# Completing the chunk inverses two heads at a time, with a stationary operand of 128 by 128

## The chip, the cores and the metric

The kernel runs on one core of one Trainium2 chip. The metric is the device time of one execution in microseconds (us), of which the median of several runs is given.

## The reference

The reference is a two-layer backbone over 2048 latent tokens and 256 context tokens with 1024 channels. The first layer projects the tokens and runs two groups of heads side by side: a bidirectional gated delta rule (four heads of 128) and grouped-query attention (four heads of 128, two key and value heads), then an output projection. The second layer is a convolution module. What the change touches is the triangular solve of the gated delta rule, which the reference writes for each chunk and head as

```python
lower = jnp.where(strict, jnp.einsum('bhnid,bhnjd->bhnij', kb, k) * decay, 0.0)
tmat = jnp.eye(GDN_CHUNK, dtype=q.dtype) + lower
u = lax.linalg.triangular_solve(tmat, v * beta[..., None], left_side=True, lower=True)
w = lax.linalg.triangular_solve(tmat, kb * jnp.exp(g)[..., None], left_side=True, lower=True)
```

followed by a scan over the chunks that carries a 128 by 128 state per head, once forward and once backward.

## The kernel before

The kernel works in stages. Projections come first. Then `gdn_products` makes the decayed products of all 18 chunks of 128 tokens and stores them in DRAM, and `gdn_subst` inverts their diagonal blocks of 32 by substitution on VectorE and GpSimd (tiles `sbC` and `sbT`); its last passes run into the next stage. That next stage, `layer0_mix`, runs attention and the delta rule side by side. The output projection and the second layer follow.

In `layer0_mix`, `merge` takes steps of two generators in turn: `attention`, and `gdn_all`, which itself alternates between the two directions d = 0 and 1. Each direction goes through the 18 chunks in its order. While `gdn_chain` does the chain of one chunk (matmuls into `pk`, `py`, `pq`, `pn`, `pa`), `gdn_inverse` completes the inverse of the next one, so there are 36 inverses in all, and `gdn_final` finishes the output of the last. The build then orders the instructions of each engine by a simulated timeline, starting from the order in which the generators emitted them; on the chip each engine works through its list in that order, and so groups of one operation can be broken up by work of another.

`gdn_inverse` holds a chunk's four heads in tiles with 128 partitions. It starts with the inverses of the diagonal blocks of 32 in `W` and doubles the block size twice (levels s = 32 and 64). At each level it forms, head by head, a product of an off-diagonal block `nt` (at level 32 a copy of its columns, `ntc`) with `X`, the transposed inverse, into PSUM tile `psq`; copies the wanted blocks out to `q = self.qz[d, s]`, whose other blocks were zeroed once in `zero_q`; multiplies by the diagonal blocks of `W` into `psw`; and writes the negated blocks back into `W`. Between the levels it transposes the 64 by 64 blocks of `W` into `pst` and copies them into a new `X`. The copies out of `psq` run on VectorE, those out of `psw` and `pst` on ScalarE. All matmuls here are fp32; each leaves two records in the trace, a transpose leaves one. Attention's matmuls use fp32 split into two F32R parts, with one record each.

All PSUM tiles of the delta rule come from the pool `ps_g` with three buffers. Attention has `ps_s` (scores, two buffers, evicted into `S` by VectorE) and `ps_t` (transposed probabilities `pt`, two buffers, read by ScalarE into `phi` and by VectorE into `plo`), and one buffer for the product `po`.

Of the kernel before, what the change touches and what calls it, by code (L numbers as in the profile page):

```python
# [8 lines left out]
F32 = mybir.dt.float32  # L9
# [5 lines left out]
PSUM = bass.MemoryType.PSUM  # L15
DRAM = bass.MemoryType.DRAM

P = 128
# [7 lines left out]
H = 4  # L26
# [80 lines left out]
class Build:  # L107
# [13 lines left out]
                return  # L121
            self.layer0_out_layer1()

# [1 line left out]
    def col(self, name, j=0, n=None):  # L125
        o, w = COLS[name]
        n = 1 if n is None else n
# [20 lines left out]
    def rsqrt(self, out, src, n):  # L148
        self.nc.gpsimd.tensor_tensor(out=out, in0=src, in1=self.mhalf[:, 0:1].to_broadcast([P, n]), op=ALU.pow)  # L149

# [1 line left out]
    def setup(self, es):  # L152
        tc, nc = self.tc, self.nc
        self.kp = kp = es.enter_context(tc.tile_pool(name="keep", bufs=1))
# [33 lines left out]
        self.d_sz = d("d_sz", [8, P, T])  # L188

    def ada_start(self, layer, conds, half, raws, pspool, ap, st):  # L190
        """Scale and shift columns {cond: (A[128,4], B[128,4])} of four channel tiles."""
        nc = self.nc
        nc_ = len(conds)
        rows = []
# [38 lines left out]
        return r  # L233

    def make_hT(self, xs, A, B, hi, lo, st, tp, cts=range(KT), bufs=3):
        """xs: token tiles [128,1024] scaled by rstd; writes hi/lo [128 ch, 8, n*128]."""
        nc = self.nc
        n = len(xs)
        for ct in cts:
            ps = tp.tile([P, 512], F32, tag="tp", name="ps_h")  # L240
            for a, x in enumerate(xs):
                nc.tensor.transpose(ps[:, a * P:(a + 1) * P], x[:, ct * P:(ct + 1) * P], self.ident)
            t = st.tile([P, 512], F32, tag="ht", name="ht", bufs=bufs)
            bias, scale = (x[:, ct:ct + 1] if not isinstance(x, list) else x[ct // 4][:, ct % 4:ct % 4 + 1] for x in (B, A))
            nc.scalar.activation(t[:, :n * P], ps[:, :n * P], AF.Identity, bias=bias, scale=scale)
            self.split(hi[:, ct, :], lo[:, ct, :], t[:, :n * P], None, nc.gpsimd if ct % 2 else nc.vector)

# [1 line left out]
    @staticmethod  # L249
    def pipe(gens):  # L250
        """Starts one generator per tick, then each older one takes a step, newest first. A generator
        that is given more than once takes a single step each time."""
        gens = list(gens)
        live = []
        for g in gens:
            if gens.count(g) > 1:
                next(g, None)
                continue
            live = [x for x in [g] + live if next(x, live) is not live]
        while live:  # L260
            live = [x for x in live if next(x, live) is not live]

    @staticmethod
    def rotate(pools):
        """Allocator over four buffers of the first pool and two of the second, in turn."""
        count = [0]

        def alloc(*a, **k):
            count[0] += 1
            last = count[0] % 6 in (0, 5)  # L270
            return pools[last].tile(*a, tag="w", bufs=2 if last else 4, **k)

        return alloc

    def ahead(self, gen, offset, steps=2):
        """gen, its first steps with a scheduling priority that lies `offset` instructions earlier."""
        for _ in range(steps):
            with self.tc.high_priority(offset):
                next(gen)
            yield  # L280
        yield from gen
# [147 lines left out]
                self.nc.sync.dma_start(self.dbg[f"{nm}{b}"], t.bitcast(F32))  # L429

    def load_w(self, src, c0, n, vec=False):
        """Weight columns [1024, n] as hi/lo half tiles of four k tiles each."""
        nc = self.nc
        his, los = [], []
        step = KT if n <= P else KT // 2
# [171 lines left out]
        return  # L607
        yield

# [1 line left out]
    def layer0_mix(self):  # L611
        tc, nc = self.tc, self.nc
        with self.es_mix as es:
# [96 lines left out]
    def zero_q(self, cp):  # L710
        nc = self.nc
        self.qz = {}
        for d in range(2):
            for s in LEVELS:
                t = cp.tile([P, H, 64], F32, name=f"qz{d}_{s}", bufs=1)
                nc.gpsimd.memset(t, 0.0)
                self.qz[d, s] = t

    # gated delta rule, chunks of 128 tokens, four heads at a time: first the decayed products of all
    # chunks and the inverses of their diagonal blocks of 32, then both directions' chains, where the  # L720
    # chain of a chunk runs beside the completion of the next one's inverse and the output of the last
    def all_products(self, gp, pp):
        for c in [16, 17, 0, 1, 2, 3, 12, 13, 14, 15] + list(range(4, 12)):
            yield from self.gdn_products(c, gp, pp)
# [90 lines left out]
        yield  # L815

    def gdn_subst(self, n, chunks):
        """Inverses of the unit triangular diagonal blocks of 32 of one group of chunks for each direction, by
        substitution: a partition (direction, block, chunk, head) holds one block. The second direction's blocks
        are transposed, so that all are upper triangular; both the inverses and their transposes are kept."""  # L820
        nc = self.nc
        B2 = BASE * BASE
        nch = len(chunks[0])
        q = nch * H
# [33 lines left out]
    def gdn_inverse(self, d, c, box):  # L858
# [5 lines left out]
        for k, t in enumerate((wc, wt)):  # L864
# [7 lines left out]
        nc.gpsimd.tensor_tensor(out=X.rearrange("p h (b i) -> p h b i", i=BASE),  # L872
                                in0=wt.unsqueeze(2).to_broadcast([P, H, 2, BASE]),
                                in1=blk[:, :, d::2, :].to_broadcast([P, H, 2, BASE]), op=ALU.mult)
        ntc = gp.tile([P, H, 64], F32, tag="ntc", name="ntc", bufs=3)
        nc.scalar.copy(ntc.rearrange("p h (b s) -> p h b s", s=BASE), nt.rearrange("p h (b t s) -> p h b t s", t=2, s=BASE)[:, :, :, 1 - d, :])
        yield
        hd, ho = (slice(64 * a, 64 * a + 64) for a in (d, 1 - d))
        for li, s in enumerate(LEVELS):
            nb = P // (2 * s)  # L880
            if li:
                pst = self.ps_g.tile([64, H, 64], F32, tag="g", name="pst")
                for h in range(H):
                    nc.tensor.transpose(pst[:, h, :], W[hd, h, hd], self.ident[hd, hd])
                X = gp.tile([P, H, 64], F32, tag="X", name="X", bufs=4)
                nc.scalar.copy(X[hd], pst)
                yield
            def blocks(t, a):
                return t.rearrange("p h (b t s) -> p h b t s", t=2, s=s)[:, :, :, a, :]

            psq = self.ps_g.tile([64, H, 64], F32, tag="g", name="psq")
            for h in range(H):
                lh, rh = (nt[hd, h, ho], X[hd, h, :]) if li else (ntc[:, h, :], X[:, h, :])
                nc.tensor.matmul(psq[:, h, :], lhsT=lh, rhs=rh, start=True, stop=True)
            q = self.qz[d, s]
            for b in range(nb):
                r, c = slice(b * s, b * s + s), slice((2 * b + 1 - d) * s, (2 * b + 2 - d) * s)
                nc.vector.tensor_copy(q[c, :, r], psq[r, :, r])
            yield
            psw = self.ps_g.tile([64, H, 64], F32, tag="g", name="psw")  # L900
            for h in range(H):
                nc.tensor.matmul(psw[:, h, :], lhsT=q[:, h, :], rhs=blocks(W, 1 - d)[:, h], start=True, stop=True)
            for b in range(nb):
                r, c = slice(b * s, b * s + s), slice((2 * b + d) * s, (2 * b + d + 1) * s)
                nc.scalar.mul(blocks(W, 1 - d)[c, :, b, :], psw[r, :, r], -1.0)
            yield
        box[key] = W

# [88 lines left out]
        nc.sync.dma_start(self.d_y[0:H, :, c * P:(c + 1) * P].rearrange("h p t -> p h t"), yt)  # L997
        yield

    # attention: units of one head and 256 queries; the scores of the next unit run beside the  # L1000
    # product with v of the current one
    KB = [(0, 0, 512), (0, 512, 512), (1, 0, 512), (1, 512, 512), (2, 0, 256)]

    def load_kv(self, kv):
# [18 lines left out]
            yield  # L1023

    def scores(self, kv, h, qp, kvt):
        """Yields after each of ten score blocks; the last value is the unit's state."""
        nc, ap = self.nc, self.ap
        scale = float(P) ** -0.5
        khi, klo = kvt[0], kvt[1]
# [103 lines left out]

        return emit

# [1 line left out]
    def ada_late(self, jobs, part_tile):  # L1137
        """Layer 1's scale and shift columns and both layers' rows of post_norm_g * gate, in small steps."""
        nc = self.nc
        for layer, blk in jobs:  # L1140
            c0 = blk * 512
# [41 lines left out]
        return G  # L1183

    def load_wout(self, src, wo, raws, eng):
        """[1024, 1024] weight as hi/lo, resident: [half][k] -> [128, 512]."""
        nc = self.nc
        his, los = [[], []], [[], []]
        for n in range(2):
# [9 lines left out]
        return his, los  # L1199

    def out_rows(self, yhi, ylo, his, los, mm, tag="mm"):
        """Two PSUM halves [128 tok, 512] of y @ W_out; yhi/ylo: k -> [128 ch, 128 tok]."""
        res = []
        for n in range(2):
            ps = mm.tile([P, 512], F32, tag=tag, name="ps_out")
# [2 lines left out]
        return res  # L1208

    def post(self, halves, gate, st, x, out=None):  # L1210
        """x + rms(halves) * gate, into x where the halves lie in PSUM and else into out, which holds the halves."""
        nc = self.nc
        ss = st.tile([P, 2], F32, tag="ss2", name="ss2")
        for n, ps in enumerate(halves):
# [299 lines left out]
```

## Time and profile before

| | |
|---|---|
| median of 3 runs | 2692.19 us (2688.54 to 2692.4) |
| the profiled execution | span 2690.4 us, from the first to the last instruction |
| TensorE | busy 2595.6 us (96%), granted clock 0.988 of full speed on average |
| VectorE, ScalarE, GpSimd | busy 75%, 50%, 53% |
| the inverses | from 894 to 1628 us of the span |

The profiled execution's own time is shown as its span alone; it lies within the spread of the three runs. Times of instructions are read from this one execution. TensorE's matmuls overlap one another and their ends are modelled, so the distance between two starts says what a matmul costs, and its own duration does not. PE is TensorE (PEld its loading of the stationary operand), DVE VectorE, ACT ScalarE, POOL GpSimd. L894 is line 894 of the kernel. A group such as `128*64 128x64` has a stationary of 128 by 64 and writes 128x64.

### The profile page before, as it was taken

The numbers are of one execution on the slowest core, as the hardware profiler recorded it, in microseconds if no ns is written. First come the engines' busy times: TensorE is split into PE (matmuls) and PEld (weight loads), VectorE is DVE, ScalarE is ACT, GpSimd is POOL, SyncE is SP. The second block draws the span as 40 slices with busy tenths as digits, with TensorE's granted clock in tenths as the row PEclk, the third lists the DMA queues.
The fourth block names the chain that finished last, engine by engine and source line by source line (L and its number), as shares of the span: only waits on it lengthen the run. The fifth ranks groups of instructions, "written<-read, shape, count | busy, mean of one in ns | idle before, by whom it ended". The sixth has DMA issues, their size and how long they took to land. (4 is left out here: it accounts for less than half of the span.)

```text
span 2690.4 us, 44112 instructions
## 1 busy us (share of the span) xinstructions
PE 2595.6 (96%) x15784; PEld 2235.1 (83%) x15784; DVE 2027.2 (75%) x4048; ACT 1357.0 (50%) x2617; POOL 1427.6 (53%) x1172
## 2 busy tenths in 40 slices
PE   7999999998899899999999999999999999999988
PEld 5888887998788688888888889888888888887867
DVE  8576667776975778776676667656379999997985
ACT  7454465223232555555555555544356767665332
POOL 3344343667776645431243332302169999997764
PEclk9999999999999999999999999999999999999999
DMA  8133334335556654444544433324411211116442
GB/s 308 50 103 101 116 118 130 111 114 147 178 170 199 167 116 109 130 115 120 148 124 122 117 103 97 112 85 135 155 49 40 71 57 62 55 59 202 159 155 98
DMA packets 372731, 323.28 MB, mean 120 GB/s; under 512 B 74784, under 2 KB 301600, under 8 KB 372512
## 3 DMA queue, kind: packets, MB, share of 16 engines
q1 hardware_dynamic: 372512, 320.46, 39.6%
q8 instruction: 125, 2.05, 0.3%
q14 instruction: 94, 0.77, 0.1%
HBM read 216.05 MB, written 104.33 MB: 119 GB/s over the span
## 5 line engine op out<-in xcount | busy, mean ns | idle before, releaser
L1392 POOL TENSOR_TENSOR ac<-ac,pr 128x512 f32<-128x512 f32 x288 | 379.3, 1340 | 22.1 <-ACT ac L1388 10.5
L1384 DVE SCALAR_TENSOR_TENSOR pc<-u,hw,pc 128x1024 f32<-128x1024 f32 x320 | 389.3, 1279 | 2.0 <-ACT pc L1382 0.7
L1095 ACT CAST phi<-pt 128x512 fp32r<-128x512 f32 x288 | 166.6, 586 | 217.5 <-PE pt L1091 207.3
L1391 ACT ACTIVATE pr<-u,hw 128x512 f32<-128x512 f32 x288 | 205.9, 722 | 124.1 <-POOL ac L1392 122.7
L1096 DVE TENSOR_TENSOR plo<-pt,phi 128x512 fp32r<-128x512 f32 x288 | 195.9, 685 | 84.1 <-ACT phi L1095 82.5
L1049 DVE TENSOR_SCALAR_CACHE_REDUCE S<-ps_s 128x512 f32<-128x512 f32 (+1 forms) x320 | 198.9, 631 | 63.3 <-PE ps_s L137 41.5
L135 PE MATMUL ps_b<-w_hi,hhi 128*128 128x256 f32 (+1 forms) x800 | 231.9, 292 | 7.3 <-DVE xn L563 5.8
L136 PE MATMUL ps_b<-w_lo,hhi 128*128 128x256 f32 (+1 forms) x800 | 228.4, 287 | 0.1
L137 PE MATMUL ps_b<-w_hi,hlo 128*128 128x256 f32 (+1 forms) x800 | 227.1, 289 | 0.6 <-POOL hlo L146 0.6
L135 PE MATMUL ps_out<-wohi,yhi 128*128 128x512 f32 x512 | 204.3, 399 | 2.2 <-DVE yhi L145 2.2
L137 PE MATMUL ps_out<-wohi,ylo 128*128 128x512 f32 x512 | 201.6, 395 | 0.6 <-DVE ylo L146 0.6
L136 PE MATMUL ps_out<-wolo,yhi 128*128 128x512 f32 x512 | 202.0, 395 | 0.0
L1058 ACT ACTIVATE S<-S,m 128x1024 f32<-128x1024 f32 (+1 forms) x192 | 177.9, 931 | 36.5 <-DVE m L1055 36.3
L846 POOL TENSOR_TENSOR sbT<-sbC 128x169 f32<-128x169 f32 (+18 forms) x76 | 122.1, 1607 | 103.9 <-DVE sbC L847 79.5
L1091 PE MATMUL pt<-ident,S 128*128 128x128 f32 x1152 | 175.5, 274 | 0.9 <-DVE plo L1096 0.9
L1119 PE MATMUL po<-phi,vhi 128*128 128x256 f32 x576 | 170.1, 317 | 3.8 <-ACT phi L1095 3.2
L135 PE MATMUL ps_a<-hhi,w_hi 128*128 128x512 f32 (+1 forms) x448 | 171.3, 382 | 0.0
L136 PE MATMUL ps_a<-hlo,w_hi 128*128 128x512 f32 (+1 forms) x448 | 170.8, 381 | 0.0
L137 PE MATMUL ps_a<-hhi,w_lo 128*128 128x512 f32 (+1 forms) x448 | 170.3, 380 | 0.2 <-POOL w_lo L146 0.2
L474 DVE SCALAR_TENSOR_TENSOR acc<-ub,cols,acc 128x512 f32<-128x512 f32 (+1 forms) x168 | 138.7, 834 | 33.8 <-POOL acc L472 32.0
L135 PEld LDWEIGHTS ps_b<-w_hi,hhi 128*128 128x128 f32 x800 | 153.9, 193 | 10.0 <-issue 4.8
L136 PEld LDWEIGHTS ps_b<-w_lo,hhi 128*128 128x128 f32 x800 | 154.0, 193 | 1.6 <-DVE w_lo L146 0.6
(323 smaller groups left out, 7699.2 us busy)
## 6 DMA issues: line engine op xcount, KB each, us to landing
raw_ada<-in_ada_w_dram SPq DMA_DIRECT2D x48, 512.0 KB
x<-in_x_dram SPq DMA_DIRECT2D x32, 512.0 KB
kq<-d_kT SPq DMA_DIRECT2D x54, 256.0 KB
raw_w<-in_ev_w_in_dram SPq DMA_DIRECT2D x26, 512.0 KB
kq<-d_qT SPq DMA_DIRECT2D x48, 256.0 KB
raw_w<-in_od_w_in_dram SPq DMA_DIRECT2D x24, 512.0 KB
d_nt<-ntA SPq DMA_DIRECT2D x36, 256.0 KB
nt<-d_nt SPq DMA_DIRECT2D x36, 256.0 KB
```

What stands on the lines that cost most here:

```text
L135: self.nc.tensor.matmul(ps, lhsT=lh, rhs=rh, start=(a == 0), stop=False)
L136: self.nc.tensor.matmul(ps, lhsT=lh, rhs=rl, start=False, stop=False)
L137: self.nc.tensor.matmul(ps, lhsT=ll, rhs=rh, start=False, stop=(a == n - 1))
L1049: nc.vector.tensor_scalar(out=S[g][:, k0:k0 + w], in0=ps[:, :w], scalar1=1.0, scalar2=None, op0=ALU.mult, op1=ALU.max, accum_out=mx[:, b:b ...
L1058: nc.scalar.activation(S[g], S[g], AF.Exp, bias=m, scale=scale, accum_out=l[:, g:g + 1])
L1091: nc.tensor.transpose(pt[:, e, a * P:(a + 1) * P], S[a][k0 // 1024][:, k0 % 1024:k0 % 1024 + P], self.ident)
L1095: nc.scalar.copy(hi, pt)
L1096: nc.vector.tensor_tensor(out=lo, in0=pt, in1=hi.bitcast(F32), op=ALU.subtract)
L1119: nc.tensor.matmul(po, lhsT=vhi[:, ks], rhs=hi[:, e, :], start=(k == 0), stop=False)
L1384: nc.vector.scalar_tensor_tensor(out=pc, in0=s(j), scalar=w(j), in1=pc, op0=ALU.mult, op1=ALU.add)
L1391: nc.scalar.mul(pr, s(j), w(j))
L1392: nc.gpsimd.tensor_tensor(out=ac, in0=ac, in1=pr, op=ALU.add)
```

## The change

`gdn_inverse` takes two heads per matmul and per transpose. The stationary operand is then always 128 by 128: the columns of two heads beside each other. Each product also holds the cross blocks of one head with the other, which are left unused. The product lands with the second head of each pair in the upper 64 partitions, so the copies out of `psq`, `pst` and `psw` are made once for the even and once for the odd heads. Two new copies on VectorE bring operands into dense form: `nto`, the columns `ho` of `nt`, at the start, and `wd`, the columns `hd` of `W`, ahead of the transposes. `X` of the second level is now one tile per direction, `self.xz[d]`, zeroed once, of which only the rows `hd` are written; its product contracts over all 128 partitions. Other parts of the diff take out comments and docstrings and are left out here.

```diff
+        self.xz = [cp.tile([P, H, 64], F32, name=f"xz{d}", bufs=1) for d in range(2)]
+        for t in self.xz:
+            nc.gpsimd.memset(t, 0.0)
...
+        hd, ho = (slice(64 * a, 64 * a + 64) for a in (d, 1 - d))
+        nto = gp.tile([P, H, 64], F32, tag="nto", name="nto", bufs=3)
+        nc.vector.tensor_copy(nto, nt[:, :, ho])
...
-        hd, ho = (slice(64 * a, 64 * a + 64) for a in (d, 1 - d))
+        pair = lambda t, e: t.rearrange("p (g e) i -> p g e i", e=2)[:, :, e, :]
+        both = lambda t, g: t[:, 2 * g:2 * g + 2, :].rearrange("p h i -> p (h i)")
...
-                pst = self.ps_g.tile([64, H, 64], F32, tag="g", name="pst")
-                for h in range(H):
-                    nc.tensor.transpose(pst[:, h, :], W[hd, h, hd], self.ident[hd, hd])
-                X = gp.tile([P, H, 64], F32, tag="X", name="X", bufs=4)
-                nc.scalar.copy(X[hd], pst)
+                pst = self.ps_g.tile([P, 2, P], F32, tag="g", name="pst")
+                wd = gp.tile([P, H, 64], F32, tag="wd", name="wd", bufs=2)
+                nc.vector.tensor_copy(wd, W[:, :, hd])
+                for g in range(2):
+                    nc.tensor.transpose(pst[:, g, :], both(wd, g), self.ident)
+                X = self.xz[d]
+                for e in range(2):
+                    nc.scalar.copy(pair(X, e)[hd], pst[64 * e:64 * e + 64, :, hd])
...
-            psq = self.ps_g.tile([64, H, 64], F32, tag="g", name="psq")
-            for h in range(H):
-                lh, rh = (nt[hd, h, ho], X[hd, h, :]) if li else (ntc[:, h, :], X[:, h, :])
-                nc.tensor.matmul(psq[:, h, :], lhsT=lh, rhs=rh, start=True, stop=True)
+            psq = self.ps_g.tile([P, 2, P], F32, tag="g", name="psq")
+            for g in range(2):
+                nc.tensor.matmul(psq[:, g, :], lhsT=both(nto if li else ntc, g), rhs=both(X, g), start=True, stop=True)
...
-                nc.vector.tensor_copy(q[c, :, r], psq[r, :, r])
+                for e in range(2):
+                    m = slice(64 * e + b * s, 64 * e + b * s + s)
+                    nc.vector.tensor_copy(pair(q, e)[c, :, r], psq[m, :, m])
...
-            psw = self.ps_g.tile([64, H, 64], F32, tag="g", name="psw")
-            for h in range(H):
-                nc.tensor.matmul(psw[:, h, :], lhsT=q[:, h, :], rhs=blocks(W, 1 - d)[:, h], start=True, stop=True)
+            psw = self.ps_g.tile([P, 2, P], F32, tag="g", name="psw")
+            for g in range(2):
+                nc.tensor.matmul(psw[:, g, :], lhsT=both(q, g), rhs=blocks(W, 1 - d)[:, 2 * g:2 * g + 2], start=True, stop=True)
...
-                r, c = slice(b * s, b * s + s), slice((2 * b + d) * s, (2 * b + d + 1) * s)
-                nc.scalar.mul(blocks(W, 1 - d)[c, :, b, :], psw[r, :, r], -1.0)
+                c = slice((2 * b + d) * s, (2 * b + d + 1) * s)
+                for e in range(2):
+                    m = slice(64 * e + b * s, 64 * e + b * s + s)
+                    nc.scalar.mul(pair(blocks(W, 1 - d)[:, :, b, :], e)[c], psw[m, :, m], -1.0)
```

## Rows read from the trace of the kernel before

**Rows 1.** The page's first part: TensorE over the whole span, busy time, share and instructions.

```profile
PE 2595.6 (96%) x15784; PEld 2235.1 (83%) x15784; DVE 2027.2 (75%) x4048; ACT 1357.0 (50%) x2617; POOL 1427.6 (53%) x1172
```

**Rows 2.** The table of stretches of the mix stage: stretch, its length, then busy time (and instructions) of PE, PEld, DVE, ACT and POOL, the granted clock, the DMA share and GB/s.

```profile
900.00:1200.00 300.00, 296.31 (x2345) 259.48 (x2342) 241.07 (x674) 171.89 (x375) 144.74 (x117) 1.00 0.50 127
1200.00:1680.00 480.00, 476.81 (x3712) 424.90 (x3712) 323.83 (x921) 265.52 (x599) 152.75 (x143) 1.00 0.41 116
900.00:1680.00 780.00, 773.12 (x6054) 684.38 (x6052) 564.89 (x1595) 437.41 (x973) 297.49 (x260) 1.00 0.45 121
...
1000.00:1050.00 50.00, 50.00 (x390) 43.92 (x390) 42.02 (x110) 27.84 (x68) 30.20 (x25) 1.00 0.39 107
```

**Rows 3.** The two longest waits of TensorE between 900 and 1680 us: who waited, for whom, us in total, times, longest.

```profile
PE ps_s L135 <- DVE S L1049: 2.6, 3, 1.5
PE psq L894 <- ACT o L949: 2.0, 1, 2.0
```

**Rows 4.** TensorE's groups with a stationary of 64 columns between 900 and 1680 us: line, operation, output and inputs, shapes, count, then busy us and mean ns of one, and the idle time before.

```profile
L902 PE MATMUL psw<-W,qz 128*64 128x64 f32 x575 | 53.4, 230 | 0.0
...
L894 PE MATMUL psq<-X,ntc 128*64 128x64 f32 x272 | 27.2, 231 | 0.0
L894 PE MATMUL psq<-X,nt 64*64 64x64 f32 x288 | 26.2, 227 | 2.0 <-ACT o L949 2.0
...
L884 PE MATMUL pst<-ident,W 64*64 64x64 f32 x144 | 13.7, 224 | 0.0
```

**Rows 5.** TensorE in order of time around 1100 us: start, time from the first start to the last end of the merged instructions, the operation and how many were merged.

```profile
1099.90 0.60 PE L1091 MATMUL pt<-ident,S 128*128 128x128 f32 x4
1100.43 0.91 PE L902 MATMUL psw<-W,qz 128*64 128x64 f32 x12
1101.27 0.39 PE L1119 MATMUL po<-phi,vhi 128*128 128x256 f32 x1
1101.49 0.28 PE L1120 MATMUL po<-phi,vlo 128*128 128x256 f32 x1
...
1102.55 0.60 PE L1091 MATMUL pt<-ident,S 128*128 128x128 f32 x4
1102.90 0.48 PE L137 MATMUL ps_s<-khi,qlo 128*128 128x512 f32 x1
1103.22 0.39 PE L135 MATMUL ps_s<-khi,qhi 128*128 128x512 f32 x1
1103.44 0.40 PE L136 MATMUL ps_s<-klo,qhi 128*128 128x512 f32 x1
...
1103.91 1.05 PE L968 MATMUL pa<-y,at 128*128 128x128 f32 x8
1104.72 0.36 PE L1119 MATMUL po<-phi,vhi 128*128 128x256 f32 x1
1104.92 0.28 PE L1120 MATMUL po<-phi,vlo 128*128 128x256 f32 x1
1105.04 0.28 PE L1119 MATMUL po<-phi,vhi 128*128 128x256 f32 x1
```

**Rows 6.** The same view around 1136 us.

```profile
1135.30 0.60 PE L1091 MATMUL pt<-ident,S 128*128 128x128 f32 x4
1135.82 0.68 PE L894 MATMUL psq<-X,nt 64*64 64x64 f32 x8
1136.43 0.94 PE L954 MATMUL pn<-y,kbd 128*128 128x128 f32 x6
1137.12 0.36 PE L1119 MATMUL po<-phi,vhi 128*128 128x256 f32 x1
1137.32 0.28 PE L1120 MATMUL po<-phi,vlo 128*128 128x256 f32 x1
```

**Rows 7.** The same view: the first and the last of the runs of narrow matmuls, 225 in all.

```profile
894.38 1.12 PE L894 MATMUL psq<-X,ntc 128*64 128x64 f32 x8
...
1627.70 0.45 PE L902 MATMUL psw<-W,qz 128*64 128x64 f32 x4
```

**Rows 8.** VectorE's groups by line and shape (columns as in rows 4): the copies out of `psq` and the casts `qhi` between 890 and 1680 us, and the same casts between 900 and 1200 us.

```profile
L898 DVE COPY qz<-psq 32x128 f32<-32x128 f32 x72 | 20.3, 282 | 7.5 <-PE psq L894 6.5
...
L898 DVE COPY qz<-psq 64x256 f32<-64x256 f32 x36 | 15.0, 415 | 8.0 <-PE psq L894 7.3
L145 DVE CAST qhi<-qr 128x256 fp32r<-128x256 f32 x28 | 13.2, 470 | 4.7 <-PE ps_s L136 4.6
...
L145 DVE CAST qhi<-qr 128x256 fp32r<-128x256 f32 x11 | 7.9, 718 | 1.5 <-PE ps_s L136 1.4
```

**Rows 9.** VectorE and GpSimd in order of time around 952 us (columns as in rows 5).

```profile
951.98 2.17 DVE L145 CAST qhi<-qr 128x256 fp32r<-128x256 f32 x1
...
951.54 2.46 POOL L846 TENSOR_TENSOR sbT<-sbC 128x841 f32<-128x841 f32 x1 [2.06 <-DVE sbC L847]
```

**Rows 10.** ScalarE's copies out of `psw` and `pst` between 890 and 1680 us (columns as in rows 4).

```profile
L905 ACT ACTIVATE W<-psw 32x128 f32<-32x128 f32 x72 | 19.2, 266 | 34.5 <-PE psw L902 33.4
...
L905 ACT ACTIVATE W<-psw 64x256 f32<-64x256 f32 x36 | 13.5, 376 | 17.9 <-PE psw L902 17.4
L886 ACT COPY X<-pst 64x256 f32<-64x256 f32 x36 | 13.2, 366 | 6.8 <-PE pst L884 6.3
```

**Rows 11.** GpSimd's zeroing of `qz` (one line of the kernel): count, duration in ns (least, median, most), first and last start in us, shape.

```profile
L716 POOL MEMSET qz<- x4: 311/311/312, 889.7 to 890.4; 128x256 f32 x4
```

## The prediction

> **What bounds the kernel now.** I read the page first: over the whole span TensorE is busy 96% of the time [rows 1], so the first question is whether it is also the bound where the edited code runs. The inverses run from about 894 to 1628 us, in the stage in which the gated delta rule and attention share the engines. The table of stretches shows TensorE busy 773.12 of the 780 us from 900 to 1680, VectorE 564.89 (72%), ScalarE 437.41 (56%) [rows 2]. TensorE waits for nobody for long there: the two largest waits are 2.6 and 2.0 us in total [rows 3]. So any TensorE time that leaves this stage should leave the span, as long as no other engine takes over. The one that could is VectorE: 241.07 us of the 300 from 900 to 1200, where the substitution of the diagonal blocks runs beside it, and 323.83 of the 480 after that [rows 2].
>
> "Busy" on TensorE hides something, though. The inverse's matmuls have a stationary 64 columns wide [rows 4], everything around them one of 128 by 128. In the order of time [rows 5, 6] I compared starts, not durations, since ends overlap. An uninterrupted 256-column matmul of attention starts 0.12 us after its neighbour (1104.92 to 1105.04), a 512-column one 0.22 (1103.22 to 1103.44). A run of 12 narrow records takes 0.84 us to the next start (1100.43 to 1101.27), a run of 8 takes 0.61 (1135.82 to 1136.43): the marginal record costs (0.84 - 0.61) / 4 = 0.058 us. Wide fp32 records cost: eight of `pa` and one 256-column successor take 1104.92 - 1103.91 = 1.01 us, less 0.12 is 0.89, 0.111 each; four transposes and one 512-column successor take 1103.22 - 1102.55 = 0.67, less 0.22 is 0.45, 0.11 each. With these prices the stretch around the run of 12, 1099.90 to 1101.49, should take 4 x 0.11 + 12 x 0.058 + 0.12 = 1.26 us; it takes 1.59, 0.33 more. Around the run of 8, 1135.30 to 1137.32: 4 x 0.11 + 8 x 0.058 + 6 x 0.111 + 0.12 = 1.69 against 2.02, again 0.33 more. The `pa` group, wide fp32 (two records to a matmul) among attention's F32R matmuls, shows no such extra, so it is the narrow stationary and not the type that costs: about 0.17 us on the way in and as much on the way out, all of it counted as busy.
>
> How often is it paid? The program's order breaks the groups up: from the first run at 894.38 to the last at 1627.70 [rows 7] the trace has 225 separate runs of narrow records. Worked in the same way for each, the median extra is 0.338 us and all together 82 us, of which some 4 are true waits for another engine: 78 us of switching.
>
> **TensorE's part of the change.** Removed: per inverse 16 records each of `psq` and `psw` and 4 of `pst`, over 36 inverses 1296 (1279 of them in the stretch of [rows 4]), at 0.058 us 75.2 us, and 78 us of switches. Added: with two heads at a time, 4 groups of 2 matmuls, two records each, and 2 transposes: 18 records, 648 in all, at 0.111 us 71.9 us. That half of each product is unused costs nothing against before, because two 64-column records at 0.058 cost what one of 128 costs. Sum: 75.2 + 78 - 71.9 = 81 us less TensorE time. The strided moving operand of `psw` is not in the trace in this width; bounds: the price of a narrow record, 0.058, and of the 128-column row, 0.111; I take 0.111, the row of the same width.
>
> [...]
>
> **VectorE's part.** `nto` and `wd` are two new SBUF copies of 128x256 per inverse, 72 in all. The nearest row is the cast `qhi` of the same size: mean 470 ns over the stage, 718 ns from 900 to 1200 [rows 8]. The spread is blocking: one took 2.17 us and ended just after GpSimd's `sbT` of 2.46 us [rows 9]. `qz` goes from 2 copies of 32x128 and 1 of 64x256 to 4 of 32x64 and 2 of 64x128. The line through 282 and 415 ns [rows 8] gives 1.04 ns a column, so 215 and 282 ns: 4 x 0.215 - 2 x 0.282 + 2 x 0.282 - 0.415 = 0.45 us more per inverse (bounds: half of the present price, no change; the present price for each, 0.98 more). Some 16.5 inverses lie in 900 to 1200: 16.5 x (2 x 0.718 + 0.45) = 31 us more, 272 in all. TensorE would need only 300 - 32 - 1 = 267 there (32 of the switching is its share). VectorE therefore becomes the bound of that stretch; the highest share it reaches in the stage is 42.02 of 50 us, with TensorE unhurt [rows 2]. I assume 95% when it is the bound: 286 us, so 14 of the 33 us are gained there and 19 given back. In the rest, 19.5 inverses at GpSimd's lighter load: 19.5 x (2 x 0.31 + 0.45) = 21 us more (0.31: the mean of the 17 casts after 1200, from 28 at 470 and 11 at 718), 345 of about 434 us, 79%. That is the share that VectorE has in 900 to 1200 now without delaying TensorE, so there the whole 44 us of switching and 2 us of records are kept.
>
> **ScalarE and GpSimd.** `W` goes from 2 x 32x128 and 1 x 64x256 to 4 x 32x64 and 2 x 64x128, and `X` from one copy to two. By the same kind of line (266 and 376 ns, [rows 10]) 0.211 and 0.266: 0.31 + 0.16, and for `X` 2 x 0.266 - 0.366 = 0.17, 0.64 us per inverse, 23 us. 460 of about 718 us stays at 64%: hidden behind TensorE. Two more zeroing writes on GpSimd cost 0.31 us each [rows 11], before the first inverse needs them; at worst 0.6 us. No DMA is added or moved.
>
> **New waits.** The second level's transposes now wait for `wd`, which waits for ScalarE's last `W` write and stands in VectorE's queue among the score copies `S` and the `plo` subtractions; behind the transposes on TensorE stand attention's matmuls. `X` of the second level is one buffer per direction in place of four; 18 inverses per direction in 734 us put the next write to it some 41 us later, so that wait is never last. At the stage's start nothing covers the longer chain: some 2 us, once.
>
> **Sum.** 14 + 44 + 2 + about 2 from the runs before 900, less 2 at the start: 60 us less than the profiled execution's 2690.4, so 2630 us. That execution lies within the runs shown (2688.5 to 2692.4, median 2692.2), so nothing is added. After the stage the work is unchanged and TensorE runs through it, so the gain is not given back later.
>
> **Rivals.**
> - *Everything is kept.* VectorE keeps pace in 900 to 1200 because substitution has slack and moves later, or the copies price nearer 0.29 us than 0.72. Gain 75 to 85 us, 2605 to 2615. For it: VectorE's share after 1200 leaves room. Against: its 272 us beside 267.
> - *VectorE binds the stage more widely.* Copies that block behind GpSimd sit ahead of `S` and `plo`, whose buffers (two each) TensorE needs back. If each of 72 costs TensorE half a microsecond more than reckoned, 36 us of the gain go, and more with `qz` at its upper bound (35 us): gain 10 to 45, 2645 to 2680.
> - *Slower: the shared PSUM pool `ps_g`.* Its three buffers are held until the last copy out of them. The copies after each inverse's five tiles grow by 0.30 + 0.15 + 0.31 + 0.16 + 0.17 = 1.1 us; if all of it stops TensorE, 39 us, and if every `wd` blocks for 2.17 us, 78 more: 117 against 81 gained, 2726. It decides from 81 / 180 = 0.45 us lost per tile. Against: TensorE's waits now are a few us in all [rows 3].
> - *No effect:* the 0.33 us belongs to the start of any group, not to the narrow shape. 2685 to 2695. Against: the `pa` group.
>
> **How the numbers follow.** Forecast (gain 45 to 75) 0.55; everything kept 0.12; VectorE more widely 0.22; no effect 0.04; slower 0.07. So faster by over 0.2% (5.4 us, about what a measurement of this kernel can tell from no change) 0.89, same 0.04, slower 0.07. The range 2606 to 2666 takes in the full gain of 84 and a gain as low as 24; the rest is the slow end. The likeliest case alone is 2615 to 2645.
>
> **What would show it.** No narrow records; 648 wide ones for the inverses; starts 0.11 us apart and the next attention matmul with no extra; the stage shorter, less in its first 300 us than after; VectorE above 90% before the substitution ends and near 80% after it. The prediction is wrong if TensorE shows new waits for `wd`, `S` or `plo` of tens of microseconds, or if the wide groups are followed by the same 0.3 us.

## The result and the profile after

The changed kernel takes 2658.31 us in the median (2655.25 to 2664.5), the kernel before 2692.30 on the same chip (2688.54 to 2693.32). The ratio is 0.9879 with a 95% interval of 0.9865 to 0.9894: 34 us less, where 60 had been forecast. The profiled execution's span falls by 35.9 us, from 2690.4 to 2654.5. The first part of the page, to be held against [rows 1]:

```profile
PE 2536.9 (96%) x15136; PEld 2217.0 (84%) x15136; DVE 2073.3 (78%) x4228; ACT 1380.5 (52%) x2761; POOL 1431.4 (54%) x1174
```

TensorE has 15784 - 15136 = 648 instructions fewer: 1296 narrow records went, 648 wide ones came. Its share stays at 96% only because the span shrank too. The table of stretches of the mix stage (columns as in [rows 2]), now cut at 1550, shortly after the last inverse:

```profile
900.00:1200.00 300.00, 286.86 (x2146) 266.62 (x2147) 267.81 (x778) 187.87 (x461) 155.15 (x129) 0.99 0.55 141
1200.00:1550.00 350.00, 343.55 (x2659) 325.90 (x2658) 276.06 (x810) 222.02 (x550) 124.96 (x115) 1.00 0.45 128
...
900.00:950.00 50.00, 48.46 (x343) 44.21 (x344) 46.87 (x142) 34.47 (x89) 36.19 (x32) 0.97 0.67 174
1100.00:1150.00 50.00, 49.06 (x376) 46.29 (x376) 47.03 (x134) 29.73 (x75) 28.56 (x24) 1.00 0.43 125
```

Before, TensorE was busy 296.31 of the first 300 us and VectorE 241.07 [rows 2]; now they are at 286.86 and 267.81. In single stretches of 50 us VectorE reaches 47.03, or 94%. TensorE has begun to wait where it did not before.

TensorE's groups with the new shape, from 900 to 1660 us (columns as in [rows 4], which they answer):

```profile
L913 PE MATMUL psw<-W,qz 128*128 128x128 f32 x288 | 45.3, 278 | 5.3 <-DVE qz L909 3.1 <-DVE r L947 1.2 <-DVE sbC L850 0.9
...
L903 PE MATMUL psq<-xz,nto 128*128 128x128 f32 x144 | 22.7, 274 | 0.0
L903 PE MATMUL psq<-X,ntc 128*128 128x128 f32 x136 | 20.6, 275 | 0.9 <-ACT W L918 0.9
...
L893 PE MATMUL pst<-ident,wd 128*128 128x128 f32 x72 | 13.2, 277 | 1.4 <-DVE wd L891 1.4
```

No record with a stationary of 64 columns is left. TensorE in order of time, at two places (columns as in [rows 5]):

```profile
1015.16 0.61 PE L913 MATMUL psw<-W,qz 128*128 128x128 f32 x4
1015.53 0.48 PE L1136 MATMUL po<-plo,vhi 128*128 128x256 f32 x2
1015.85 0.60 PE L1104 MATMUL pt<-ident,S 128*128 128x128 f32 x4
...
1304.91 0.61 PE L903 MATMUL psq<-X,ntc 128*128 128x128 f32 x4
1305.27 0.48 PE L135 MATMUL ps_s<-khi,qhi 128*128 128x512 f32 x1
1305.59 0.40 PE L136 MATMUL ps_s<-klo,qhi 128*128 128x512 f32 x1
```

From 1015.16 to 1015.85 there are 0.69 us; four wide records and two of 256 columns cost 4 x 0.111 + 2 x 0.12 = 0.68. From 1304.91 to 1305.59 there are 0.68; 4 x 0.111 + 0.23 = 0.67. The 0.33 us that stood around each narrow run is gone, so the switching that the prediction read out of [rows 5, 6] was there and the change removes it. The question is why some 81 us of freed TensorE time became 36.

**Where TensorE's time went.** To see small waits I priced every TensorE record of a stretch at its undisturbed distance to the next start (0.228 us for 512 columns, 0.119 for 256, 0.111 for 128, 0.058 for a narrow record) and took the sum from the stretch's length. What remains is switching, waiting, and matmuls that ran while the granted clock was lower. In before it is 101.2 us from 880 to the end of attention at 1815; 82 of these lie at narrow runs (78 switching, 4 waits), so about 23 are not switching. In after 71 us remain from 880 to 1850, none of it switching. Most of both is waits; some 5 us of before's 23 and 10 of after's 71 are matmuls in short spells of 3.4 to 10.3 us at a granted clock of 0.50. The longest of them in after is from 1799 to 1809 us, after waits of TensorE of up to 2.38 us. There the starts of 512-column records are 0.43 us apart in place of 0.228:

```profile
1799.20:1809.50 10.30, 8.47 (x23) 5.71 (x24) 7.33 (x14) 5.57 (x9) 4.41 (x4) 0.50 0.64 206
...
1805.14 0.63 PE L137 MATMUL ps_out<-wohi,ylo 128*128 128x512 f32 x1
1805.57 0.63 PE L135 MATMUL ps_out<-wohi,yhi 128*128 128x512 f32 x1
```

By this count the span should fall by 101.2 - 71 + 3.3 (wide for narrow records) = 33.5 us; it falls by 35.9. Of the 81 us freed, 48 came back, 4 of them as matmuls at the lower clock and the others as new waits. For the stretches of after and of the experiments described below (us; before's hold the switching too):

```
                      880-900  900-1200  1200-1550  1550-1650  1650-1750  1750-1850
before                   11.8      35.8       38.3        8.3        6.7        0.3
after                    12.8      26.1       11.5        9.5        0.4       10.4
e5_copies_twice          11.2      38.8       19.6        1.0        5.4        6.8
e2_copies_scalar         11.0      20.0        6.6       11.6        0.4        3.8
e7_steps430              12.7      19.4        6.0       10.6        0.6        6.3
e6_qz_split              12.1      16.8        6.1        7.1        0.2        0.2
e8_qz_scalar             12.2      16.2        3.9        7.0        0.0        5.5
e9_whole_transpose       11.7      18.2        4.9        8.5        0.4        0.4
```

Before's 35.8 from 900 to 1200 hold 3.7 us of waits and 32 of switching, and its 1200 to 1630 hold 46.6 us, of which 2.7 are waits. So after loses anew about 22 us from 900 to 1200 (3 of them at the lower clock), 9 from 1200 to 1550, and 13 at the stage's end (20.3 against some 7 in before).

Whom TensorE waits for, from 900 to 1660 us (columns as in [rows 3]):

```profile
PE ps_s L135 <- DVE S L1062: 8.4, 9, 4.0
PE po L1132 <- ACT phi L1108: 5.5, 8, 2.2
PE po L1136 <- DVE plo L1109: 4.0, 7, 1.0
PE psw L913 <- DVE qz L909: 3.1, 1, 3.1
PE pst L893 <- DVE wd L891: 1.4, 1, 1.4
```

The largest is for VectorE's score copies `S`, 8.4 us where it had been 2.6 [rows 3]; `wd` itself is waited for 1.4 us only. The view shows some 28 us in few waits, the pricing by distance some 47 from 900 to 1650: many waits are gaps of half a microsecond, as at 1019 us, where the gap from 1018.77 to 1019.62 is 0.85 in place of 0.23:

```profile
1018.77 0.40 PE L137 MATMUL ps_s<-khi,qlo 128*128 128x512 f32 x1
1019.62 1.16 PE L952 MATMUL py<-r,W 128*128 128x128 f32 x8 [0.45 <-DVE r L947]
```

and VectorE beside it, without a gap of its own:

```profile
1018.00 0.53 DVE L850 TENSOR_REDUCE sbC<-sbT 128x19 f32<-128x361 f32 x1
1018.44 1.12 DVE L947 SCALAR_TENSOR_TENSOR r<-pk,negc,vt 128x128 f32<-128x128 f32 x4
```

The delta rule's product waits for `r`. The last matmuls into its input `pk` had started at 1014.94, so `r` had stood in VectorE's queue behind other work. VectorE's new or changed groups, 890 to 1660 us (they answer [rows 8]):

```profile
L909 DVE COPY qz<-psq 32x64 f32<-32x64 f32 x144 | 31.6, 220 | 5.4 <-PE psq L903 2.0 <-PE ps_s L137 1.0
...
L891 DVE COPY wd<-W 128x256 f32<-128x256 f32 x36 | 22.2, 620 | 1.5 <-ACT W L918 1.4
...
L909 DVE COPY qz<-psq 64x128 f32<-64x128 f32 x72 | 20.7, 287 | 2.2 <-PE psq L903 1.0
...
L880 DVE COPY nto<-nt 128x256 f32<-128x256 f32 x36 | 15.2, 421 | 0.5
```

The added work is 22.2 + 15.2 + (31.6 + 20.7 - 20.3 - 15.0) = 54 us; the prediction had 31 + 21 = 52.

### The profile page after: what moved, and what is told of

The parts are those of the page before. It is cut to its first block, busy times and chain, and to the rows that moved or that the text cites. A ratio compares the mean times of both kernels' runs of the same rounds, so it can differ in the third digit from the quotient of the medians.

```text
span 2654.5 us, 43188 instructions
## 1 busy us (share of the span) xinstructions
PE 2536.9 (96%) x15136; PEld 2217.0 (84%) x15136; DVE 2073.3 (78%) x4228; ACT 1380.5 (52%) x2761; POOL 1431.4 (54%) x1174
## 5 line engine op out<-in xcount | busy, mean ns | idle before, releaser
L1109 DVE TENSOR_TENSOR plo<-pt,phi 128x512 fp32r<-128x512 f32 x288 | 195.3, 685 | 74.6 <-ACT phi L1108 71.9
```

Of the source, the lines that this page charges most:

```text
L1109: nc.vector.tensor_tensor(out=lo, in0=pt, in1=hi.bitcast(F32), op=ALU.subtract)
```

## The experiments

Three theories stood against each other. **V**: the gain is lost to VectorE's fuller queue, in proportion to the work added there. **H**: it is lost to hand-offs, since each inverse's chain has more and later copies, on whatever engine. **E**: it is lost at the stage's end, because the delta rule finishes earlier against attention, which is then left alone. The delta rule's last `pa` moves from 1655 to 1583 us (72 earlier), attention's last `po` only from 1815 to 1792.

One thing changes in nearly every experiment besides its edit: the build orders each kernel anew. Of the pairs of instructions outside the inverses that stand beside each other from 880 to 1830 us, after keeps about four in five on TensorE in e2 and e5, and about half on VectorE. No run holds the order fixed, so a single difference can be partly that of the order; what speaks for a theory is that several kernels line up.

**e1_narrow_copies.** Before, with all the copies of the change, while every matmul and transpose stays 64 wide:

```diff
+        nto = gp.tile([P, H, 64], F32, tag="nto", name="nto", bufs=3)
+        nc.vector.tensor_copy(nto, nt[:, :, ho])
...
+                wd = gp.tile([P, H, 64], F32, tag="wd", name="wd", bufs=2)
+                nc.vector.tensor_copy(wd, W[:, :, hd])
-                    nc.tensor.transpose(pst[:, h, :], W[hd, h, hd], self.ident[hd, hd])
+                    nc.tensor.transpose(pst[:, h, :], wd[hd, h, :], self.ident[hd, hd])
...
-                nc.vector.tensor_copy(q[c, :, r], psq[r, :, r])
+                for e in range(2):
+                    nc.vector.tensor_copy(pair(q, e)[c, :, r], pair(psq, e)[r, :, r])
```

`nto` is the second level's stationary, one head at a time, and `X` and `W` are copied in halves in the same way. 

> The kernel before, with the matmuls left narrow, but with every copy of the change: nto and wd on VectorE, and the copies out of psq, pst and psw made once for the even and once for the odd heads. It prices the copies by themselves. Theory V (the change frees some 80 us of TensorE and VectorE's extra work, 54 us in its trace, takes part of it back): TensorE still pays its switches and leaves VectorE room, so 2695 to 2706 us, with VectorE near 90% from 900 to 1200. Rival H (what is lost is the longer hand-over from engine to engine in each inverse, whatever the load): the same hand-overs cost the same 25 to 35 us here, 2715 to 2727. Rival E (it is lost at the end of the stage, where attention is left alone): no change, 2690 to 2695.

Measured: 2693.46 us (2691.1 to 2698.91) against 2692.21, ratio 0.9999 (0.9985 to 1.0013). The stretch from 900 to 1200:

```profile
900.00:1200.00 300.00, 295.70 (x2332) 258.00 (x2331) 256.09 (x747) 173.98 (x438) 142.82 (x116) 1.00 0.50 127
```

VectorE has risen from 241.07 to 256.09 us, 85%, and the time has not moved: H's number is far off, V's lower end of 2695 missed by a little, and E's number (no change) is met. The copies cost nothing as long as TensorE pays for its switches. V's explanation is that the switches give the other engines time to catch up; this run does not show that by itself. Since such a cover would hide hand-offs as well as VectorE's work, the next kernels have to tell V from H without it.

**e2_copies_scalar.** After, with the two new copies on ScalarE:

```diff
-        nc.vector.tensor_copy(nto, nt[:, :, ho])
+        nc.scalar.copy(nto, nt[:, :, ho])
...
-                nc.vector.tensor_copy(wd, W[:, :, hd])
+                nc.scalar.copy(wd, W[:, :, hd])
```

> The changed kernel, with nto and wd copied by ScalarE in place of VectorE; nothing else differs. Theory V: VectorE loses 37 us of work and ScalarE, at 64%, takes it without delay: 10 to 18 us faster than the changed kernel, 2640 to 2648. Rivals H and E: as many hand-overs and the same end, so 2653 to 2662.

Measured: 2644.31 us (2641.99 to 2647.93), ratio 0.9822 (0.98 to 0.9844), 14 us below after. V's number; H and E expected no move. The chain has as many copies as in after, on another engine. By itself this run does not part V from H, as a `wd` copy also takes less time on ScalarE (the last section), 0.2 us for each of 36; e5 is to do that. The stretch from 900 to 1200:

```profile
900.00:1200.00 300.00, 289.38 (x2193) 270.47 (x2194) 258.92 (x764) 205.15 (x508) 156.20 (x130) 0.99 0.56 144
```

**e3_psw_only.** Before, with only the hunk of `psw` taken over (tile, two matmuls, `W` written per head of a pair); everything else stays narrow:

```diff
-            psw = self.ps_g.tile([64, H, 64], F32, tag="g", name="psw")
-            for h in range(H):
-                nc.tensor.matmul(psw[:, h, :], lhsT=q[:, h, :], rhs=blocks(W, 1 - d)[:, h], start=True, stop=True)
+            psw = self.ps_g.tile([P, 2, P], F32, tag="g", name="psw")
+            for g in range(2):
+                nc.tensor.matmul(psw[:, g, :], lhsT=both(q, g), rhs=blocks(W, 1 - d)[:, 2 * g:2 * g + 2], start=True, stop=True)
...
```

> The kernel before, with psw alone taken two heads at a time (ScalarE's copies split, nothing added on VectorE). Theory V: the runs of narrow records with psw, 89 or more of 225, fall away, 89 x 0.338 = 30 us, and all of it is kept since VectorE has no more to do: 2658 to 2667, as much as the whole change gained. If the extra 0.33 us were not the narrow stationary's: 2690 to 2695. Rival H: no hand-over is added, so the same as V. Rival E: half is lost at the end, 2672 to 2680.

Measured: 2657.94 us (2650.49 to 2662.84), ratio 0.9862 (0.9832 to 0.9892): as much as the whole change. The trace has 131 narrow runs left, 94 fewer, with 43.6 us of extra in all (median 0.336). 94 x 0.338 = 32 us were to be freed and 34 were gained. The kernel holds both kinds of group side by side:

```profile
1100.23 0.61 PE L904 MATMUL psw<-W,qz 128*128 128x128 f32 x4
1100.60 0.48 PE L1127 MATMUL po<-plo,vhi 128*128 128x256 f32 x2
1100.92 0.60 PE L1095 MATMUL pt<-ident,S 128*128 128x128 f32 x4
...
1107.65 0.40 PE L137 MATMUL ps_s<-khi,qlo 128*128 128x512 f32 x1
1107.98 0.35 PE L886 MATMUL pst<-ident,W 64*64 64x64 f32 x3
1108.27 0.66 PE L1095 MATMUL pt<-ident,S 128*128 128x128 f32 x4
```

Around the wide group nothing is lost (0.69 us for 0.68 of work). The three narrow transposes come 0.33 us after a 512-column matmul that needs 0.23, and their successor follows 0.29 us after three records of 0.058: about 0.1 lost on each side here. The forecast's price per run holds for the median. Nor does this kernel lose at the stage's end (9.5 us after 1550 by the same pricing, 1.5 of them switching, against before's 7), although its last `pa` comes 37 us earlier than before's: E's number is missed too.

**e4_psw_psq32.** The same with `psq` of the first level paired too, and its `qz` copies split as in the change:

```diff
+            if li:
+                psq = self.ps_g.tile([64, H, 64], F32, tag="g", name="psq")
+                for h in range(H):
+                    nc.tensor.matmul(psq[:, h, :], lhsT=nt[hd, h, ho], rhs=X[hd, h, :], start=True, stop=True)
+            else:
+                psq = self.ps_g.tile([P, 2, P], F32, tag="g", name="psq")
+                for g in range(2):
+                    nc.tensor.matmul(psq[:, g, :], lhsT=both(ntc, g), rhs=both(X, g), start=True, stop=True)
...
```

> As the one with psw alone, and psq of the first level two heads at a time as well: no new copies of nt or W, VectorE's qz copies of the first level split (11 us more). Narrow are left psq and pst of the second level. Theory V: 143 runs x 0.338 = 48 us, less some 3 for VectorE: 2644 to 2652, faster than the whole change. Rival H: 4 to 8 us are lost to the split copies, 2650 to 2656. Rival E: 2665 to 2672.

Measured: 2655.82 us (2652.25 to 2661.32), ratio 0.9865 (0.984 to 0.9891). 97 narrow runs are left, 128 fewer, 128 x 0.338 = 43 us freed, 36 gained. V expected at most 2652 and missed by 4 us. The intervals of e3 and e4 overlap: the second pairing, worth 11 us of switching, gained nothing that these runs can measure. They cannot rule it out either: the two profiled executions, e3's slowest and e4's fastest, are 11 us apart (2660.9 and 2649.9). That its `qz` copies on VectorE took the gain is V's reading, not shown.

**e5_copies_twice.** After, with two further copies on VectorE that nobody reads:

```diff
+        nto2 = gp.tile([P, H, 64], F32, tag="dum", name="nto2", bufs=1)
+        nc.vector.tensor_copy(nto2, nt[:, :, ho])
...
+                wd2 = gp.tile([P, H, 64], F32, tag="dum", name="wd2", bufs=1)
+                nc.vector.tensor_copy(wd2, W[:, :, hd])
```

> The changed kernel, with nto and wd each copied a second time by VectorE into a tile that nobody reads: 37 us more work on VectorE at the rows of the changed kernel, no hand-over more. Theory V (VectorE's load from 900 us on takes the gain back): 12 to 25 us slower than the changed kernel, 2668 to 2682, with VectorE above 92% from 900 to 1200. Rival H (the length of the hand-over, not the load): 2654 to 2663, as the changed kernel. Rival E (the end of the stage): the same, 2654 to 2663.

Measured: 2670.22 us (2666.07 to 2674.49), ratio 0.9918 (0.9894 to 0.9942), 12 us above after. Nothing depends on these copies, so no chain of copies is longer: apart from the new order, what they cost is laid here to VectorE's fuller queue. In groups of that kernel's trace they add 20.9 + 20.8 us of VectorE time, and TensorE's remainder rises by 13 us from 900 to 1200 and 8 from 1200 to 1550, of which 7 return at the end of the stage (13.2 after 1550 for 20.3).

```profile
L882 DVE COPY nto<-nt 128x256 f32<-128x256 f32 x36 | 20.9, 581 | 0.3
L895 DVE COPY wd<-W 128x256 f32<-128x256 f32 x36 | 20.8, 577 | 0.0
```

(L882 and L895 are the dummies.)

**e6_qz_split.** e2, with the odd heads' `qz` copies on ScalarE too:

```diff
-                    nc.vector.tensor_copy(pair(q, e)[c, :, r], psq[m, :, m])
+                    (nc.scalar.copy if e else nc.vector.tensor_copy)(pair(q, e)[c, :, r], psq[m, :, m])
```

> The kernel with nto and wd on ScalarE, and the qz copies of the odd heads on ScalarE as well: 26 us less on VectorE, none less in number. Theory V: 3 to 8 us faster than with nto and wd alone, 2636 to 2642. Rivals H and E: no change, 2642 to 2648.

Measured: 2632.92 us (2624.85 to 2634.89), ratio 0.9774 (0.9752 to 0.9797). V's number or a little better. This version beats both kernels, and it comes out where the forecast for the change was. But V explains only part of it: of the 11 us by which e6's remainder is below e2's, 3.7 lie from 900 to 1550, where the copies run, and 8 after 1550.

**e7_steps430.** e2, with the number of steps lowered over which the planner lays out the delta rule against attention's 865, so that its instructions are spread later among attention's:

```diff
-GDN_STEPS = 500
+GDN_STEPS = 430
```

> The kernel with nto and wd on ScalarE, and GDN_STEPS 430 for 500, so that steps of the delta rule are emitted more slowly beside attention and the rule ends later. Rival E: attention is no longer left alone as long at the end of the stage, the idle time of TensorE from the end of the delta rule to the end of attention falls from 13 to some 7 us: 2636 to 2641. Theory V alone: 2642 to 2648.

Measured: 2643.54 us (2639.68 to 2647.42), ratio 0.982 (0.9798 to 0.9842): e2's time, so E's number is missed. But the edit did not do what E needed: the delta rule's last `pa` starts at 1580.3 us against 1581.6 in e2, so its end is not set by this number. The order of TensorE's instructions is that of e2 almost one by one, so e7 is a repeat of e2, and E is left untried by it. What differs between the two after 1750 (3.8 and 6.3 us) is about the 2.7 us that e7 lost in a spell of 6.8 us at a granted clock of 0.50, from 1788 on, which e2 did not have.

**e8_qz_scalar.** e6 with all `qz` copies on ScalarE:

```diff
-                    (nc.scalar.copy if e else nc.vector.tensor_copy)(pair(q, e)[c, :, r], psq[m, :, m])
+                    nc.scalar.copy(pair(q, e)[c, :, r], psq[m, :, m])
```

> The kernel with nto, wd and the odd heads' qz copies on ScalarE, and now the even heads' qz copies there too: 26 us less on VectorE, as much more on ScalarE, which goes from 222 of 300 us (900 to 1200) to some 235. Theory V, at the slope so far (12 us for 37 more, 25 for 63 less): 5 to 10 us faster, 2622 to 2629. If ScalarE has become as scarce as VectorE (whichever of the two is fuller delays TensorE): no gain or a loss, 2631 to 2642.

Measured: 2635.94 us (2634.08 to 2638.01) against 2691.20, ratio 0.9794 (0.9779 to 0.981): no better than e6. The straight line of V (less VectorE work, less time) ends here for the whole time. e6 and then e8, 900 to 1200:

```profile
900.00:1200.00 300.00, 290.73 (x2208) 273.96 (x2209) 245.10 (x710) 222.14 (x569) 154.34 (x127) 0.99 0.54 139
```

```profile
900.00:1200.00 300.00, 293.77 (x2220) 274.00 (x2219) 234.76 (x649) 234.14 (x627) 154.57 (x129) 1.00 0.57 142
```

VectorE and ScalarE are level at 234 us in e8. The remainder from 900 to 1200 hardly changes (16.8 and 16.2); from 1200 to 1550 it still falls, from 6.1 to 3.9, and from 1750 to 1850, where none of these copies run, it rises from 0.2 to 5.5. So the loss against V's number lies at the stage's end. That ScalarE has become scarce is not shown.

**e9_whole_transpose.** e6 without `wd`: four transposes of 128 by 128 of `W` in place of two of pairs, and `X` by one ScalarE copy:

```diff
-                nc.scalar.copy(wd, W[:, :, hd])
-                for g in range(2):
-                    nc.tensor.transpose(pst[:, g, :], both(wd, g), self.ident)
+                for h in range(H):
+                    nc.tensor.transpose(pst[:, h, :], W[:, h, :], self.ident)
...
-                for e in range(2):
-                    nc.scalar.copy(pair(X, e)[hd], pst[64 * e:64 * e + 64, :, hd])
+                nc.scalar.copy(X[hd], pst[hd, :, hd])
```

> The kernel with the odd heads' qz copies on ScalarE, with wd left out: W is transposed as it lies, four whole heads of 128 by 128 in place of two pairs of halves, and X is taken from it by one ScalarE copy. TensorE does 2 transposes more per inverse at 0.11 us, 8 us in all; ScalarE loses some 0.4 + 0.17 us per inverse, 20 us; the hand-over from ScalarE's W to the transposes loses one copy. If TensorE is the bound: 5 to 8 us slower, 2637 to 2642. If the hand-over or ScalarE's load holds TensorE up (rival H): 0 to 6 us faster, 2627 to 2633.

Measured: 2645.5 us (2637.69 to 2647.21), ratio 0.9822 (0.9798 to 0.9846), 12.6 above e6. The 72 more transposes cost 72 x 0.111 = 8 us of TensorE time, and the hand-off and two ScalarE copies that each inverse is spared give nothing visible back: H's number (at most 2633) is missed by 12 us, that of a bound TensorE (at most 2642) by 4. The 4 us beyond the 8 lie within the spread of the two kernels' runs.

## Why the prediction was half right

**Switching (right).** 225 runs at 0.338 us. Those runs are gone in after without an extra around the wide groups, and e3 gained 34 us for the 32 that its 94 runs fewer were worth. "No effect" is refuted. Only the split was misread: not 0.17 us on the way in and as much on the way out, but 0.09 and 0.25 in the median, as the rows around 1100 us already show (0.09 and 0.24); the sum does not use it. In before's trace a change of stationary shape thus costs time on both sides, 0.09 us going into a narrow run and 0.25 coming out; what TensorE does in that time no run shows.

**Price of the wide records (right).** 648 records at 0.111 us, `psw` with its strided moving operand included, leave no residue in the two stretches above. Replacing narrow by wide cost nothing: 71.9 us of wide records for 75.2 of narrow ones.

**VectorE's added work (right).** 54 us for 52. The mean of `wd`, 620 ns, is a mixture:

```profile
L891 DVE COPY wd<-W x36: 269/289/2669, 902.9 to 1531.3; 128x256 f32<-128x256 f32 x36
```

that is least, median and most in ns.

**900 to 1200 (number right, picture not).** The forecast let TensorE lose 19 us there because VectorE would be the bound at 95%. It lost about 22, 3 of them at the lower clock, with VectorE at 89%. VectorE never became the bound of the stretch as a whole; TensorE waits already with VectorE 89% full, since at single moments what it needs stands behind other work, as at 1019 us.

**1200 on (wrong).** The step "79%: that is the share that VectorE has in 900 to 1200 now without delaying TensorE, so there the whole 44 us are kept" failed. VectorE was at 276.06 of 350 us, 79% as forecast, and TensorE still had about 9 us of new waits. The share had been harmless under another condition: TensorE spent 32 of those 300 us on switches. With the switches in place e1 had VectorE at 85% at no cost. e2 and e5 show what is paid without the switches, 14 us less for the 37 us of VectorE work moved away and 12 more for 42 added, some 0.3 to 0.4 us for each. The remainders from 900 to 1550, where the copies run, line up by VectorE's work over five kernels: 58.4 us in e5, 37.6 in after, 26.6 in e2, 22.9 in e6 and 20.1 in e8. So over these five kernels the cost of a fuller VectorE is a slope and not a threshold, and the slope flattens: 0.5 us for each added in e5, then 0.3, and 0.1 for the last two moves.

**"The gain is not given back later" (wrong).** Some 13 us are lost anew between 1550 and 1850. From 1550 to 1750, while attention runs to its end, there are only some 2 of them (9.9 against about 7.8 without the switching in before). The other 10 lie from 1792 to 1810 us, after attention's last product at 1792.3, where the next stage begins with transposes into `ps_h`:

```profile
1792.38 2.79 PE L242 MATMUL ps_h<-ident,x 128*128 128x128 f32 x24
1797.55 0.66 PE L242 MATMUL ps_h<-ident,x 128*128 128x128 f32 x4 [2.38 <-ACT ht L245]
```

In before, only eight of these transposes stood together there, and the output projection's matmuls followed without a gap:

```profile
1814.81 1.04 PE L242 MATMUL ps_h<-ident,x 128*128 128x128 f32 x8
1815.61 0.47 PE L135 MATMUL ps_out<-wohi,yhi 128*128 128x512 f32 x1
```

The waits for ScalarE's `ht` are 4.6 us in the view, and 3.4 us more went to the spell at the lower clock that followed. By these rows most of this loss belongs to what the order leaves for TensorE at the end of the stage, and little of it to attention being left alone, theory E. In e6, 16 of the transposes stand together there without a wait, and the loss is 0.2 us. Why the order comes out so in one kernel and not in another is open.

**Sum.** Forecast 60 us, less 3 (900 to 1200), 9 (to 1550) and 13 (the end), gives 35; measured 34 to 36. The time lies in the stated range, but outside the likeliest case (2615 to 2645). The case that came is the second rival, VectorE binding more widely (2645 to 2680). Its mechanism, TensorE waiting for `S` and `plo`, holds for the inverses' stretch and not for the stage's end, and the long `wd` copies (up to 2669 ns) are not all of it: moving half of the `qz` copies, which take only 175 to 296 ns in after, took another 3.7 us off the remainder there. The prediction's sign of being wrong, new waits for `wd`, `S` or `plo` of tens of microseconds, came out at 10 us in the view (13.8 from 900 to 1660 against 3.7), more by distances. The slower rival did not come; what part the PSUM pool has in the waits was not isolated.

## What to carry to other kernels

Count how often a run of odd-shaped matmuls is entered and left, and price it by distances between starts: here a busy TensorE hid a tenth of the stage, 78 of 780 us, and pairing `psw` alone, 94 of the 225 runs, gave as much as the whole edit. When TensorE's time falls, price the work that it had covered anew: a share of VectorE that cost nothing before is no evidence for afterwards (85% from 900 to 1200 at no cost in e1, 79% from 1200 to 1550 with some 9 us of new waits in after). Then spread the new copies over the engines: here it paid until VectorE and ScalarE were about equally full (245 and 222 of 300 us in e6), and the one step beyond gained nothing that could be measured. And look at the end of the stage by itself: 13 of the 48 us were lost there, after the last inverse.

## What the hardware showed unasked

The same copy of 128 by 256 takes 269 to 2669 ns on VectorE (above), and 397 to 420 on ScalarE. From e6:

```profile
L891 ACT COPY wd<-W x36: 397/406/420, 912.7 to 1531.0; 128x256 f32<-128x256 f32 x36
```

The long ones lie beside GpSimd. Of the 36 copies in after, 15 took over 0.5 us; each of them started while a GpSimd instruction was running and ended about 0.15 us after that instruction did. The other 21 took 269 to 295 ns, although three of them started during a GpSimd instruction too. An example is this pair of after, the VectorE row first and then the GpSimd row:

```profile
956.20 2.22 DVE L891 COPY wd<-W 128x256 f32<-128x256 f32 x1
...
955.70 2.57 POOL L849 TENSOR_TENSOR sbT<-sbC 128x900 f32<-128x900 f32 x1 [1.35 <-DVE sbC L850]
```

The copy ends at 958.42, 0.15 us after GpSimd's instruction at 958.27. ScalarE's 36 copies of `wd` in e6 show no such spread (397 to 420 ns), nor do those in e2 (402 to 409). Why the long copies last until GpSimd's instruction is over is not shown by a run. On ScalarE the mean is lower (406 against 620 ns) although VectorE's least is lower still (269).
